# Three Strassen pieces instead of two in the first down product, nine low parts made by adding DMAs

## The chip, the cores and the metric

The kernel runs on one core of one Trainium2 chip. The metric is device time in microseconds (us) of one execution. Engine names are those of the profile: PE (matrix multiply), PEld (its weight load), DVE (vector), ACT (scalar), POOL (GpSimd), SP (the queue that issues most loads).

## The reference

One hybrid decoder layer for 256 tokens of width 1024 in float32: a SwiGLU feed-forward, a mixer (Mamba-2 and differential attention side by side), a second SwiGLU, each with RMSNorm before and after. What the change touches is the last product of the first feed-forward:

```python
D_MODEL, SEQ, D_FF = 1024, 256, 2816

def swiglu(x, w_gate, w_up, w_down):
    return (jax.nn.silu(x @ w_gate) * (x @ w_up)) @ w_down

h = h + 0.5 * rmsnorm(swiglu(rmsnorm(h, ffn1_pre_g[l]), ffn1_w_gate[l], ffn1_w_up[l], ffn1_w_down[l]),
                      ffn1_post_g[l])
```

So 256 x 2816 activations meet a 2816 x 1024 weight (the "down product"); the second feed-forward does the same with its own weights.

## The kernel before, in words

**Precision.** PE multiplies in a rounded float32 (`F32R`). Each weight and each activation is split into a high part (`hi`, the rounded value) and a low part (`lo`, the remainder), and each product is three: hi x hi, lo x hi, hi x lo. ACT makes `hi` by a cast, DVE makes `lo` by a subtraction (`whi`/`wlo` L250/L253 for ordinary pieces, `wqh`/`wql` L130/L135 for Strassen pieces).

**Weights.** They come in 1 MB pieces into three buffers called `raw` (SP issues the loads in order, L229); when the last reader of a buffer is done, the next piece is loaded. The split parts go into 4 KB buffers (`k4`, 29 of them). `take(ahead)` hands the split parts of the next unit to PE and first has the units ahead of it split: three pieces ahead, where a piece counts four and one Strassen product one, so twelve Strassen products ahead.

**The down product.** The 2816 rows are eleven pieces of 256 rows ("p"). An ordinary piece takes 24 matmuls of 128 x 512: two 128-row halves, two token blocks, two column halves, three terms. Two neighbouring pieces (512 rows) can be taken together as one "quad" (`q`) by Strassen's algorithm in Winograd's form: the 2 x 2 block product is made with seven products instead of eight, 42 matmuls instead of 48. For this a quad needs four sums of weight quarters (`wt`, L122, on DVE) and four sums of activations (`sums_of`, L607 to L610, made in the gate and up loop and split there). Three of the seven products (1, 2, 3) use a weight quarter as it is (`PLAIN`); four (5, 6, 7, 4) use a sum. `FIRST = (1, 2, 3, 5, 7, 6, 4)` is the order of the products of a quad, `LAST = (1, 6, 7, 2, 5, 3, 4)` that of the last one. The string `DOWN` says which pieces form quads: `"p q1 p p q2 p ppp"` in the first feed-forward (`f1`), `"q1 p q2 p q3 ppp"` in the second (`f2`). The last three pieces are held back (`TAIL = 3`): they are multiplied for token block 0 first, then for block 1, so that the norm of block 0 runs beside the matmuls of block 1.

**Order of the work.** PE follows the program in the stretches marked `own_order(PE)`, the tail of the down product among them; elsewhere a scheduler lays the instructions of each engine out when the program is built. On the chip each engine then follows its own list in order. After the last quad, `combine` (L654 to L657) adds the products: a copy of product 1 from its bank by ACT (`p1`, L657), then additions on DVE. `post_norm` scales the result (`og`, L541, with the gain row `pg`, loaded on POOL's queue at L554), POOL computes the reciprocal root (L447, L448), DVE updates `h` (L550), and PE transposes the new `h` for the next norm (`pu_mx`, L456).

Of the kernel before, what the change touches and what calls it, by code (L numbers as in the profile page):

```python
# [16 lines left out]
F32 = mybir.dt.float32  # L17
F32R = mybir.dt.float32r
AF = mybir.ActivationFunctionType
ALU = mybir.AluOpType  # L20
# [7 lines left out]
T = 256  # L28
# [16 lines left out]
QK_US = 2.4  # L45
GATE_US = 1.75
SSD_US = 1.55
DOWN = {"f1": "p q1 p p q2 p ppp", "f2": "q1 p q2 p q3 ppp"}
FIRST, LAST = (1, 2, 3, 5, 7, 6, 4), (1, 6, 7, 2, 5, 3, 4)
BREAK, STOP = object(), object()  # L50

# [2 lines left out]
def tile_hybrid_layer(ctx: ExitStack, tc: tile.TileContext, x, ffn1_pre_g, ffn1_w_gate, ffn1_w_up,  # L54
# [4 lines left out]
    nc = tc.nc  # L59
# [5 lines left out]
    def k4(shape, name, dt=F32):  # L65
        return sb.tile(shape, dt, tag="k4", name=name, bufs=K4_BUFS)
# [24 lines left out]
    last_lo = [None]  # L91

    class Quad:
# [3 lines left out]
        PLAIN = {1: 0, 2: 2, 3: 3}  # L97
        SUMS = {5: (1, 0), 6: (3, 5), 7: (3, 1), 4: (2, 6)}

        def __init__(self, i, products):  # L100
            self.i, self.sums, self.products = i, {}, products
            self.uses = [[p for p in products if p in (1, 5)], [p for p in products if p in (5, 7)],
                         [p for p in products if p in (2, 4)], [p for p in products if p in (3, 6, 7)]]

# [21 lines left out]
        def split(self, p):  # L126
            load_to(self.i + 2)
            hi = k4([P, 2, 512], f"wqh{self.i}{p}", F32R)
            src = self.quarter(self.PLAIN[p], p) if p in self.PLAIN else self.sum_of(p)
            nc.scalar.copy(hi, src)  # L130
            for later in self.products[self.products.index(p) + 1:][:1]:
                if later in self.SUMS:
                    self.sum_of(later)
            lo = k4([P, 2, 512], f"wql{self.i}{p}", F32R)
            last_lo[0] = nc.vector.tensor_sub(lo, src, hi.bitcast(F32)).ins  # L135
            self.give_back()
            return lambda kt: hi[:, kt, :], lambda kt: lo[:, kt, :]

# [2 lines left out]
    chunks, units = [], []  # L141
# [5 lines left out]
    def t_chunk(w, k0, c0):  # L147
        chunk(w[k0:k0 + D, c0:c0 + T].rearrange("(j p) c -> p j c", p=P), [P, KD, T])

    def s_chunk(w, k0, c0):  # L150
        chunk(w[k0:k0 + 512, c0:c0 + 512].rearrange("(j p) c -> p j c", p=P), [P, 4, 512])

    def n_chunk(w, k0):
        chunk(w[k0:k0 + 2 * P, :].rearrange("(j p) c -> p j c", p=P), [P, 2, D])

    def quad(w, k0, products):

        n = len(units)
        for k in (k0, k0 + 2 * P):
            n_chunk(w, k)  # L160
        del units[n:]
        q = Quad(len(chunks) - 2, products)
        units.extend((q, p) for p in products)


    down, QUADS = {}, {}
    for tag, plan in DOWN.items():
        QUADS[tag] = [int(c) for c in plan if c.isdigit()]
# [11 lines left out]
    def ffn_chunks(tag, wg, wu, wd):  # L180
        for w in (wg, wu):
            for k0 in (0, 512):
                s_chunk(w[0], k0, 0)
        for j in range(2, FF // T):
            t_chunk(wg[0], 0, j * T)
            t_chunk(wu[0], 0, j * T)
        for kind, j in down[tag]:
            if kind == "q":
                quad(wd[0], j * 2 * T, LAST if j == QUADS[tag][-1] else FIRST)
            else:  # L190
                n_chunk(wd[0], j * T)

    ffn_chunks("f1", ffn1_w_gate, ffn1_w_up, ffn1_w_down)
    for c in range(2):
        for k0 in (0, 512):
# [19 lines left out]
    for c in range(4):  # L215
        n_chunk(w_out[0], c * 2 * P)
    ffn_chunks("f2", ffn2_w_gate, ffn2_w_up, ffn2_w_down)

    raws, splits = [], []
    taken = [0]  # L220

    def load_to(n):
        while len(raws) < min(n, len(chunks)):
            i = len(raws)
            src, shape = chunks[i]
            r = sb.tile(shape, F32, tag="raw", name=f"raw{i}", bufs=RAW_BUFS)
            nj = shape[1] // 4 if i == 0 else shape[1] // 2 if i < 4 else shape[1]
            for j in range(0, shape[1], nj):
                nc.sync.dma_start(r[:, j:j + nj, :], src[:, j:j + nj, :])  # L229
            raws.append(r)  # L230
# [296 lines left out]
    def set_u(b, us):  # L527
        for q in range(2):
            split(*in_u(b)(q), us[q])
# [70 lines left out]
    def sums_of(g, even, odd):  # L600


        bs = (slice(0, P), slice(P, T))
        v = k4([P, 4, 2, P], f"sv{g}")
        hi, lo = ((k3 if g < 3 else k4)([P, 3, 2, P], f"s{n}{g}", F32R) for n in "hl")
        more = k2([P, 2, 2, P], f"s4{g}", F32R)
        nc.vector.tensor_tensor(v[:, 0], even[:, :, bs[1]], odd[:, :, bs[1]], ALU.add)  # L607
        nc.vector.tensor_sub(v[:, 2], even[:, :, bs[0]], even[:, :, bs[1]])
        nc.vector.tensor_sub(v[:, 1], v[:, 0], even[:, :, bs[0]])
        nc.vector.tensor_sub(v[:, 3], odd[:, :, bs[0]], v[:, 1])  # L610
        split(hi, lo, v[:, 0:3])
        split(more[:, 0], more[:, 1], v[:, 3])
        return ([hi[:, i] for i in range(3)] + [more[:, 0]], [lo[:, i] for i in range(3)] + [more[:, 1]])
# [724 lines left out]
    for c in range(4):  # L1338
# [3 lines left out]
        o = (c % 2) * 2  # L1342
# [134 lines left out]
```

## Time and profile before

| | |
|---|---|
| median of 3 runs | 738.33 us (738.31 to 738.46) |
| the profiled execution | 737.54 us, of which the span is 735.8 us |
| mean granted PE clock in it | 0.997 |
| busy: PE, DVE, ACT, POOL | 726.4, 591.9, 462.1, 38.6 us |
| first down product on PE | from 132.36 us |
| DMA: hardware queue q1, software queue q0 | 129.51 MB, 7.22 MB |

The span runs from the first to the last instruction. A matmul's listed duration includes its pipeline, so matmuls overlap: what a matmul costs is read from the distance of starts, or from the length of a stretch and the number of matmuls in it. `out<-in` names tiles with their numbers left out. "f1p" and "f2p" mark the banks of the two down products.

### The profile page before, as it was taken

The numbers are of one execution on the slowest core, as the hardware profiler recorded it, in microseconds if no ns is written. First come the engines' busy times: TensorE is split into PE (matmuls) and PEld (weight loads), VectorE is DVE, ScalarE is ACT, GpSimd is POOL, SyncE is SP. The second block draws the span as 40 slices with busy tenths as digits, with TensorE's granted clock in tenths as the row PEclk, the third lists the DMA queues.
The fourth block names the chain that finished last, engine by engine and source line by source line (L and its number), as shares of the span: only waits on it lengthen the run. The fifth ranks groups of instructions, "written<-read, shape, count | busy, mean of one in ns | idle before, by whom it ended". The sixth has DMA issues, their size and how long they took to land.

```text
span 735.8 us, 10869 instructions
## 1 busy us (share of the span) xinstructions
PE 726.4 (99%) x4211; PEld 628.1 (85%) x4211; DVE 591.9 (80%) x904; ACT 462.1 (63%) x777; POOL 38.6 (5%) x72
## 2 busy tenths in 40 slices
PE   8999999999999999999999999999999999999996
PEld 6888888888889999999888788888888888888874
DVE  7978768998677878787996998785784878779994
ACT  7657556665566565958975577782663657566562
POOL 2700000000300000000000000000010000000000
PEclk9999999999999999999999999999999999999998
DMA  8884674469353647567464664475470765664541
GB/s 299 229 261 150 218 229 171 155 216 348 118 172 117 201 143 226 192 188 226 146 219 154 202 222 138 152 238 191 127 241 34 229 199 153 222 217 143 188 168 57
DMA packets 94212, 137.96 MB, mean 187 GB/s; under 512 B 2684, under 2 KB 68304, under 8 KB 94160
## 3 DMA queue, kind: packets, MB, share of 16 engines
q1 hardware_dynamic: 91488, 129.51, 54.2%
q0 software_dynamic: 2368, 7.22, 3.1%
q8 instruction: 33, 0.54, 0.3%
q10 hardware_dynamic: 304, 0.53, 0.2%
q14 instruction: 19, 0.16, 0.1%
HBM read 136.17 MB, written 1.08 MB: 187 GB/s over the span
## 4 chain that ended last, share of the span: by engine, by line
PE 97%; DVE 2%; issue 1%; DMA 0%; ACT 0%; DVEq 0%
PE pup_f L316 9%; PE pg_f L316 9%; PE pgt L335 6%; PE pws L335 6%; PE acc_f1p L625 5%; PE acc_f2p L625 4%; PE pg_f L315 4%; PE pup_f L315 4%; PE pn_f L335 3%; PE pn_mx L335 3%; PE acc_mx L573 3%; PE pn_f L345 3%; PE pwd L335 3%; PE acc_f1p L573 3%; PE pz L302 2%; PE pxs L304 2%
## 5 line engine op out<-in xcount | busy, mean ns | idle before, releaser
L253 DVE TENSOR_TENSOR wlo<-raw,whi 128x1024 fp32r<-128x1024 f32 (+1 forms) x226 | 266.6, 1208 | 22.7 <-ACT whi L250 21.7
L250 ACT CAST whi<-raw 128x1024 fp32r<-128x1024 f32 (+1 forms) x225 | 226.2, 1044 | 18.1 <-DMA raw<-in_w_in_dram 3.8
L316 PE MATMUL pup_f<-u_f,whi 128*128 128x512 f32 x288 | 101.3, 396 | 0.0
L316 PE MATMUL pg_f<-u_f,whi 128*128 128x512 f32 x288 | 101.2, 396 | 0.0
L315 PE MATMUL pg_f<-u_f,wlo 128*128 128x256 f32 x252 | 70.6, 280 | 0.0
L315 PE MATMUL pup_f<-u_f,wlo 128*128 128x256 f32 x252 | 70.3, 279 | 0.0
L316 PEld LDWEIGHTS pup_f<-u_f,whi 128*128 128x128 f32 x288 | 52.8, 188 | 9.8
L316 PEld LDWEIGHTS pg_f<-u_f,whi 128*128 128x128 f32 x288 | 52.8, 188 | 9.6
L315 PEld LDWEIGHTS pg_f<-u_f,wlo 128*128 128x128 f32 x252 | 47.5, 188 | 1.7
L315 PEld LDWEIGHTS pup_f<-u_f,wlo 128*128 128x128 f32 x252 | 47.5, 189 | 1.6
L321 DVE TENSOR_TENSOR su_f<-pup_f,su_f 128x256 f32<-128x256 f32 x36 | 15.1, 420 | 26.0 <-ACT su_f L320 25.8
L130 ACT CAST wqh<-wt 128x1024 fp32r<-128x1024 f32 x20 | 21.0, 1052 | 23.2 <-DVE wt L122 23.2
L320 ACT COPY su_f<-pup_f 128x256 f32<-128x256 f32 x36 | 13.4, 373 | 35.1 <-PE pup_f L316 34.9
L335 PE MATMUL pgt<-whi,u_mx 128*128 128x512 f32 x128 | 33.1, 393 | 0.0
L301 PE MATMUL pxs<-u_mx,whi 128*128 128x256 f32 x128 | 31.7, 285 | 0.0
L302 PE MATMUL pz<-u_mx,whi 128*128 128x256 f32 x128 | 31.6, 284 | 0.0
L301 PE MATMUL pz<-u_mx,whi 128*128 128x256 f32 x128 | 31.6, 284 | 0.0
L302 PE MATMUL pxs<-u_mx,whi 128*128 128x256 f32 x128 | 31.4, 283 | 0.0
L335 PEld LDWEIGHTS pgt<-whi,u_mx 128*128 128x128 f32 x128 | 23.6, 188 | 5.4 <-issue 0.7
L1009 DVE SCALAR_TENSOR_TENSOR xs<-pxs,cols_b,xs 128x255 f32<-128x255 f32 (+2 forms) x48 | 21.9, 475 | 6.3 <-ACT xs L1006 5.9
L291 ACT CAST gh_f<-sg_f 128x512 fp32r<-128x512 f32 x18 | 11.2, 622 | 21.5 <-DVE sg_f L771 21.5
L302 PEld LDWEIGHTS pz<-u_mx,whi 128*128 128x128 f32 x128 | 24.5, 192 | 0.2 <-issue 0.2
(397 smaller groups left out, 1698.5 us busy)
## 6 DMA issues: line engine op xcount, KB each, us to landing
raw<-in_w_in_dram SPq DMA_DIRECT2D x40, 1024.0 KB, 5.4
raw<-in_ffn_w_down_dram SPq DMA_DIRECT2D x22, 1024.0 KB, 4.9
raw<-in_ffn_w_gate_dram SPq DMA_DIRECT2D x20, 1024.0 KB, 5.6
raw<-in_ffn_w_up_dram SPq DMA_DIRECT2D x20, 1024.0 KB, 5.4
raw<-in_ssd_w_branch_dram SPq DMA_DIRECT2D x8, 1024.0 KB, 5.3
acb<-acd POOLq DMA_DIRECT2D x8, 512.0 KB, 5.5
raw<-in_da_w_branch_dram SPq DMA_DIRECT2D x4, 1024.0 KB, 5.1
raw<-in_w_out_dram SPq DMA_DIRECT2D x4, 1024.0 KB, 5.0
```

The costliest lines, as they stand in the source:

```text
L130: nc.scalar.copy(hi, src)
L250: copy(hi[:, js, :], r[:, q * nj + j:q * nj + j + n, :])
L253: nc.vector.tensor_sub(lo[:, js, :], r[:, q * nj + j:q * nj + j + n, :], hi[:, js, :].bitcast(F32))
L301: nc.tensor.matmul(acc[m], wh(j)[:, cs], ah(k0 + j), start=first and j == ks[0], stop=False)
L302: nc.tensor.matmul(acc[m], wh(j)[:, cs], al(k0 + j), start=False, stop=False)
L315: nc.tensor.matmul(acc[:, :T], wl(j)[:, cs], ah(j), start=False, stop=False)
L316: nc.tensor.matmul(acc, wh(j)[:, cs], ahl(j), start=j == 0, stop=j == KD - 1)
L335: nc.tensor.matmul(acc, a(k0 + j), b(j), start=first and i == 0, stop=last and i == 11)
L345: nc.tensor.matmul(accs[b], x_(k0 + j), w_(j), start=first and j == 0 and w_ is wh and x_ is acts[b][0], stop=last and j == 3 and w_ is wl)
L573: nc.tensor.matmul(acc[b][q], x_[:, ts], w_(kt)[:, halves[q]], start=begin and i == 0 and kt == 0 and x_ is ah and w_ is wh, stop=i == n - ...
L625: nc.tensor.matmul(bank[p], x_, w_, start=p not in begun, stop=last and p in (1, 5, 6, 7))
L1009: nc.vector.scalar_tensor_tensor(dst[:, m, s:], acc[:, m, :T - s], cw(3 - s, c), dst[:, m, s:], ALU.mult, ALU.add)
```

## The change

`DOWN["f1"]` becomes the same plan as for `f2`: three quads instead of two, and the first quad at the start. So one more pair of ordinary pieces (48 matmuls) is taken as a quad (42), with its four weight sums and four activation sums, and the quads stand at other places.

For quads of `f1` the low part of the products 1, 2 and 3 is made in another way: ACT writes `-hi` into `lo` (one more activation of 128 x 1024 each), and a DMA on POOL's queue adds the weight quarter to it, read once more from DRAM (512 KB each, nine in all). The DVE subtraction of these nine is gone. The low parts of products 5, 6, 7 and 4 are still made by DVE, and the second feed-forward is not changed.

```diff
-DOWN = {"f1": "p q1 p p q2 p ppp", "f2": "q1 p q2 p q3 ppp"}
+DOWN = {"f1": "q1 p q2 p q3 ppp", "f2": "q1 p q2 p q3 ppp"}
+ADDING = ("f1",)
...
             lo = k4([P, 2, 512], f"wql{self.i}{p}", F32R)
-            last_lo[0] = nc.vector.tensor_sub(lo, src, hi.bitcast(F32)).ins
+            if self.adding and p in self.PLAIN:
+
+                nc.scalar.activation(lo, hi.bitcast(F32), AF.Copy, scale=-1.0)
+                j, o = divmod(self.PLAIN[p], 2)
+                nc.gpsimd.dma_start(lo, chunks[self.i + j][0][:, :, o * 512:(o + 1) * 512], accum_op=ALU.add)
+            else:
+                last_lo[0] = nc.vector.tensor_sub(lo, src, hi.bitcast(F32)).ins
             self.give_back()
...
-    def quad(w, k0, products):
+    def quad(w, k0, products, adding):
...
-                quad(wd[0], j * 2 * T, LAST if j == QUADS[tag][-1] else FIRST)
+                quad(wd[0], j * 2 * T, LAST if j == QUADS[tag][-1] else FIRST, tag in ADDING)
```

More of the change, by code (lines that the diff above doesn't have):

```diff
@@ L98, in tile_hybrid_layer, with __init__ @@
         SUMS = {5: (1, 0), 6: (3, 5), 7: (3, 1), 4: (2, 6)}
-        def __init__(self, i, products):
-            self.i, self.sums, self.products = i, {}, products
+        def __init__(self, i, products, adding):
+            self.i, self.sums, self.products, self.adding = i, {}, products, adding
             self.uses = [[p for p in products if p in (1, 5)], [p for p in products if p in (5, 7)],
@@ L161, in quad @@
         del units[n:]
-        q = Quad(len(chunks) - 2, products)
+        q = Quad(len(chunks) - 2, products, adding)
         units.extend((q, p) for p in products)
```

## The prediction

> **What bounds the kernel now.** I read the page first, then PE's waits, then PE stage by stage.
>
> ```profile
> PE 726.4 (99%) x4211; PEld 628.1 (85%) x4211; DVE 591.9 (80%) x904; ACT 462.1 (63%) x777; POOL 38.6 (5%) x72
> ...
> PE 97%; DVE 2%; issue 1%; DMA 0%; ACT 0%; DVEq 0%
> ```
>
> PE is busy for 99% of the span and holds 97% of the chain that ended last. PE's waits (us in total, times, longest):
>
> ```profile
> PE warm L411 <- POOL ident L397: 1.6, 1, 1.6
> PE pn_f L345 <- DVE raw_u L464: 0.3, 1, 0.3
> PE pn_f L345 <- DVE whi L250: 0.3, 1, 0.3
> PE pu_f L456 <- DMA h<-in_x_dram: 0.2, 1, 0.2
> ```
>
> These are all the waits it has, and none lies in a down product or a gate and up loop. So the weights are ready in time everywhere, a matmul less is worth its full pace, and any new wait of PE is a loss in full. Next, the windows of the first down product (second column the length, then PE, PEld, DVE, ACT, POOL busy, clock, DMA share, GB/s):
>
> ```profile
> 137.81:147.49 9.68, 9.68 (x43) 7.90 (x42) 9.19 (x9) 5.94 (x7) 0.00 (x0) 1.00 0.56 198
> 147.49:158.37 10.88, 10.88 (x49) 9.01 (x48) 9.60 (x9) 5.21 (x6) 0.00 (x0) 1.00 0.58 209
> ...
> 132.00:168.00 36.00, 36.00 (x159) 29.55 (x158) 33.08 (x33) 21.27 (x24) 0.53 (x1) 1.00 0.63 217
> 163.00:170.00 7.00, 7.00 (x32) 5.70 (x31) 7.00 (x8) 4.46 (x5) 0.53 (x1) 1.00 0.96 336
> ```
>
> The first row is a quad (42 matmuls), the second two ordinary pieces (48).
>
> **The matmuls.** A quad in place of two pieces: 10.88 - 9.68 = 1.20 us less on PE. That is all the change can give, since PE waits for nothing else that it could remove. It is 0.16% of the time, under the 0.2% (1.5 us) that a measurement of this kernel can tell from no change.
>
> **The engines beside PE.** Costs of one instruction:
>
> ```profile
> L250 ACT CAST whi<-raw 128x1024 fp32r<-128x1024 f32 x222 | 224.4, 1050 | 17.9 <-DMA raw<-in_w_in_dram 3.8 <-DMA raw<-in_ffn_w_down_dram 3.8 <-DMA raw<-in_ffn_w_up_dram 3.7
> L135 DVE TENSOR_TENSOR wql<-raw,wqh 128x1024 fp32r<-128x1024 f32 x15 | 18.2, 1219 | 3.6 <-ACT wqh L130 3.6
> ```
>
> DVE for the down weights: before 2 quads x 11 (4 sums, 7 lows) + 7 pieces x 2 = 36; after 3 x 8 + 5 x 2 = 34, two fewer, 2.4 us. ACT: before 2 x 7 + 7 x 2 = 28; after 3 x 10 + 5 x 2 = 40, twelve more, 12.6 us at 1.05 (the new copy is bounded by this cast of its shape). The stretch 132 to 168 leaves ACT 36 - 21.3 = 14.7 us idle, so ACT becomes nearly full but stays below PE. The third set of activation sums in the loop costs nothing: the second feed-forward's loop has the same three, and no row of PE's waits names it. If that cover failed it would cost at most its DVE time, some 3 us by my estimate.
>
> **What an adding DMA takes.** No run so far has one. The nearest rows (KB, us from issue to landing; the last two answers are the single transfers issued at 305.96 and 306.92):
>
> ```profile
> raw<-in_ffn_w_down_dram SPq DMA_DIRECT2D x22, 1024.0 KB, 4.9
> acb<-acd POOLq DMA_DIRECT2D x8, 512.0 KB, 5.5
> pg_mx<-in_mix_post_g_dram POOLq DMA_DIRECT2D x1, 512.0 KB, 3.7
> ```
> ```profile
> DMA to landing us min/median/max: 4.0/5.5/7.1
> ```
> ```profile
> 305.96 0.53 POOL L1071 DMA_DIRECT2D acb<-acd  x1 [16.16 <-PE pz L302]
> 306.92 0.53 POOL L1071 DMA_DIRECT2D acb<-acd  x1 [0.43 <-PE pz L302]
> ```
> ```profile
> DMA to landing us min/median/max: 4.0/4.0/4.0
> ```
> ```profile
> DMA to landing us min/median/max: 5.1/5.1/5.1
> ```
>
> A plain 512 KB on POOL's queue lands after 3.7 (quiet) to 7.1 (beside loads). An add also has to read what stands in the tile, so I take it as two passes. A second pass costs 4.9 - 3.7 = 1.2 us quiet; of the pair, the second landed at 312.0, the first at 310.0, so 2.0 us under load. Ends: 3.7 (adding costs nothing) and 7.1 + 2.0 = 9.1. Quiet two passes give 4.9, busy ones 4.0 + 2.0 = 6.0; I take 5.5, between them and the plain median. Below 3.7 nothing speaks for: it moves no less than the plain one.
>
> [...]
>
> **Third quad, product 3: a new chain.** In the order of instructions of the changed program, ACT's copy of product 1 out of its bank (`p1`, L657) stands ahead of the -hi copy for product 3 of the last quad, whose DMA waits for that copy. So this low part cannot be begun before PE has finished product 1 of the same quad. The second feed-forward has the same PE order (LAST: 1, 6, 7, 2, 5, 3, 4) and the same copy:
>
> ```profile
> 703.54 0.39 PE L625 MATMUL acc_f2p<-wql,gh_f 128*128 128x512 f32 x1
> ...
> 709.69 0.39 PE L625 MATMUL acc_f2p<-wql,s 128*128 128x512 f32 x1
> ```
> ```profile
> 703.97 0.59 ACT L657 COPY p_f<-acc_f2p 128x512 f32<-128x512 f32 x1 [0.38 <-PE acc_f2p L625]
> 704.45 1.05 ACT L130 CAST wqh<-raw 128x1024 fp32r<-128x1024 f32 x1
> ```
>
> Product 1 ends at 703.93, the copy starts at 703.97, the next ACT instruction (there the cast, here -hi) at 704.45 and ends at 705.5; the DMA is issued at about 705.6, and PE wants the low part at 709.69. That leaves 4.1 us. With 5.5 us PE waits 1.4 (ends 0 and 5.0). On POOL only the load of the gain row is queued behind it. It is read late in the tail and hidden: `pg` went out at 708.1 in the second feed-forward and was read at 718.5.
>
> ```profile
> L554 POOL DMA_DIRECT2D pg_f<-in_ffn_post_g_dram x2: 533/580/626, 163.0 to 708.1; - x2
> ```
> ```profile
> 718.53 0.69 DVE L541 TENSOR_TENSOR og_f<-p_f,pg_f 128x512 f32<-128x512 f32 x1
> ```
>
> **Second quad, products 1 to 3.** ACT starts them behind `gh_f` of the last loop step:
>
> ```profile
> 679.25 0.62 ACT L291 CAST gh_f<-sg_f 128x512 fp32r<-128x512 f32 x1 [2.98 <-DVE sg_f L771]
> 679.77 2.94 ACT L130 CAST wqh<-raw 128x1024 fp32r<-128x1024 f32 x3
> ```
> ```profile
> 690.48 0.39 PE L625 MATMUL acc_f2p<-wql,s 128*128 128x512 f32 x1
> ```
>
> DVE has three subtractions fewer ahead of this point, but it waits for casts that ACT now makes three copies later, so I leave the start where it is. Now six ACT instructions stand there at 0.98 us (2.94 / 3): the DMAs go out at about 681.7, 683.7 and 685.7. PE wants the third low part at 690.48, 4.8 us after. The three queue on one another: at two quiet passes of 1.2 us each, the last lands at 681.7 + 5.5 + 2 x 2.4 = 692.0, and PE waits 1.5 us. Ends: 0 (plain pace, 685.7 + 3.7 = 689.4) and 5.2 (two passes of 2.0 us each: 681.7 + 6.0 + 8.0 = 695.7). The first quad's adds have more room:
>
> ```profile
> 661.99 1.05 ACT L130 CAST wqh<-raw 128x1024 fp32r<-128x1024 f32 x1
> ```
> ```profile
> 675.36 0.39 PE L625 MATMUL acc_f2p<-wql,s 128*128 128x512 f32 x1
> ```
>
> The third cast starts at 661.99; with itself, three -hi copies and one `gh_f` (0.62) its DMA goes out by 666.8, 8.5 us before PE's use at 675.36: hidden up to that.
>
> **The tail.** DVE's order there changes: between the last addition of block 0 and the update of `h`, two `wlo` subtractions now stand where there was none.
>
> ```profile
> 181.99 0.68 DVE L785 TENSOR_TENSOR u_f<-acc_f1p,u_f 128x512 f32<-128x512 f32 x1
> 182.70 0.69 DVE L541 TENSOR_TENSOR og_f<-u_f,pg_f 128x512 f32<-128x512 f32 x1
> 184.60 1.41 DVE L550 SCALAR_TENSOR_TENSOR h<-og_f,rp_f,h 128x512 f32<-128x512 f32 x2 [1.21 <-POOL rp_f L448]
> ```
> ```profile
> 185.81 1.03 PE L456 MATMUL pu_mx<-ident,h 128*128 128x128 f32 x8
> ```
>
> Two at some 1.14 us (starts apart) are 2.3; the idle 1.2 before `h` hides half, and `h` is later by 1.1. Its second half is ready at 186.0 now and PE takes it up at about 186.3, so PE waits 0.8 us (ends 0 and 1.5, where a weight load is late too).
>
> **Sum.** -1.2 + 1.5 + 1.4 + 0.8 = +2.5 us. Against the profiled execution, 737.54, that is 740.0; the median lies 0.8 above it (738.33), so 740.8.
>
> **Rivals.**
> - *The adds land in time.* At 4.1 us or less neither place waits, and PE loses at most the 0.8 of the tail: 737.1 to 737.9, faster than before, by less than can be told. It is decided at product 3 of the last quad. For it: 3.7 for a quiet load and 4.0 for some beside others. Against it: the median of 5.5 and the second read. [...] 0.26.
> - *The DMA engines become the bound.* Each add at two busy passes; the share was 0.63 over the down product and 0.96 around 163 to 170, where the last adds meet the loads of the next pieces. Waits of 5.2 and 5.0, with 0.8 for the tail, give +9.8: up to 748. For it: the 0.96. Against it: over 132 to 168 a third of the engines' time is free. 0.17.
> - *It gives more than the matmuls*, by an easier tail: over 1.5 us less, 736.5. PE's waits leave no room for it. 0.04.
> - *The change does not do what it says*: the instruction lists show nine DMAs on POOL and the six matmuls gone, so I give it no chance of its own.
>
> **How the numbers follow.** The forecast's own case (adds of 4.3 to 6.5 us, waits at both places or at the last) has 0.53 and reaches from 738.3 to 743.5; its likeliest point is 740.8. A fifth of it lies under 739.8, within 0.2%. So same: 0.26 + 0.11 = 0.37; faster by over 0.2%: 0.04; slower: 0.42 + 0.17 = 0.59. The range for 8 in 10 takes in the rival below and half of the one above: 737.2 to 745.5.
>
> **What would show it.** In the profile after: waits of PE on a DMA into `wql` (`acc_f1p`, L625's successor), one at product 3 of the last quad with the DMA's issue right behind ACT's `p1` copy, and one in the second quad; an issue-to-landing time of the adding DMA over 4.1 us; DVE's `h` later against `u_f` in the tail, with PE waiting at `pu_mx`; a quad stretch of 9.7 us plus these waits. I am wrong if the adds land under 4 us, if the scheduler's lists leave `p1` free of that -hi copy, or if raw loads come late enough that ACT's casts and not the adds hold PE.

## The result, and the profile after

The changed kernel takes 746.16 us (median of 6 runs; the kernel before 738.24 in the same runs): a ratio of 1.0123, 95% interval 1.0098 to 1.0149. It is slower by 8 us where the forecast was 2.5 us (740.8, range to 745.5). The six runs went from 744.96 to 754.3 us; the longest had the lowest mean granted clock (0.988), the two shortest the highest (0.998). Its profiled execution took 746.76 us with a span of 745.1, 9.3 us more than the span of before. Lines of the changed program stand seven further down (L625 is L632 now).

The page of the kernel after (busy time, DMA queue of POOL, chain, issue to landing):

```profile
PE 728.6 (98%) x4205; PEld 628.3 (84%) x4205; DVE 592.8 (80%) x908; ACT 474.3 (64%) x791; POOL 50.7 (7%) x81
...
q0 software_dynamic: 4816, 11.94, 7.0%
...
PE 87%; issue 4%; DMA 3%; DVE 3%; POOL 1%; ACT 1%; SPq 0%; DVEq 0%; POOLq 0%; ACTq 0%
...
wql<-in_ffn_w_down_dram POOLq DMA_DIRECT2D x9, 512.0 KB, 7.6
```

The six matmuls are gone (4211 to 4205), yet PE is busy 2.2 us longer: some of its matmuls got slower (listed with 0.63 us instead of 0.39 between 157.17 and 159.73 us). The chain holds DMA now, and an adding DMA lands after a median of 7.6 us. PE's waits in the kernel after (us in total, times, longest):

```profile
PE acc_f1p L632 <- DMA wql<-in_ffn_w_down_dram: 6.5, 4, 1.8
PE warm L418 <- POOL ident L404: 1.6, 1, 1.6
PE pu_mx L463 <- DVE h L557: 0.8, 1, 0.8
```

Its timeline, the PE rows that waited:

```profile
149.45 0.50 PE L632 MATMUL acc_f1p<-wql,gh_f 128*128 128x512 f32 x1 [1.26 <-DMA wql<-in_ffn_w_down_dram]
...
152.80 0.50 PE L632 MATMUL acc_f1p<-wql,gh_f 128*128 128x512 f32 x1 [1.69 <-DMA wql<-in_ffn_w_down_dram]
...
156.23 0.50 PE L632 MATMUL acc_f1p<-wql,s 128*128 128x512 f32 x1 [1.78 <-DMA wql<-in_ffn_w_down_dram]
...
178.97 0.50 PE L632 MATMUL acc_f1p<-wql,s 128*128 128x512 f32 x1 [1.74 <-DMA wql<-in_ffn_w_down_dram]
...
194.59 1.32 PE L463 MATMUL pu_mx<-ident,h 128*128 128x128 f32 x8 [0.80 <-DVE h L557]
```

Three waits in the second quad (all three plain products), one at product 3 of the third, one in the tail: the places of the forecast, which had reckoned with one wait in the second quad. The second quad's three additions are issued 2.0 us apart and land after 8.2, 9.5 and 10.9 us:

```profile
141.24 1.19 POOL L140 DMA_DIRECT2D wql<-in_ffn_w_down_dram  x1 [13.77 <-ACT wql L138]
143.28 1.18 POOL L140 DMA_DIRECT2D wql<-in_ffn_w_down_dram  x1 [0.85 <-ACT wql L138]
145.30 1.19 POOL L140 DMA_DIRECT2D wql<-in_ffn_w_down_dram  x1 [0.84 <-ACT wql L138]
```

Between the first two, at 142.26 us, SP issues a plain load of 1 MB (`raw`), which lands after 8.6 us. What the forecast did not have is in the windows from the second of these waits on (length, PE, PEld, DVE, ACT, POOL busy, granted clock, DMA share, GB/s):

```profile
149.50:152.80 3.30, 1.61 (x7) 1.00 (x7) 3.28 (x3) 2.11 (x3) 0.00 (x0) 1.00 1.12 220
152.80:156.20 3.40, 1.65 (x6) 1.05 (x6) 2.46 (x3) 2.94 (x3) 0.00 (x0) 1.00 1.08 300
156.20:158.00 1.80, 1.77 (x5) 1.43 (x6) 0.59 (x1) 0.00 (x0) 1.18 (x1) 0.67 1.02 385
158.00:160.00 2.00, 2.00 (x6) 1.58 (x5) 1.86 (x2) 0.00 (x0) 0.00 (x0) 0.50 1.07 367
160.00:162.00 2.00, 2.00 (x9) 1.59 (x9) 1.60 (x2) 1.34 (x2) 0.00 (x0) 0.94 0.96 181
```

The DMA engines are full through the whole stretch, at only 220 GB/s in its first row (the loads alone moved 336 GB/s at a share of 0.96 before). And after the third wait PE's granted clock falls to 0.50. From 156.56 to 160.16 us PE starts 9 matmuls in 3.6 us instead of 2.0.

The loss up to the first matmul of the next projection (`pn_mx`, 190.82 us before, 199.89 after, so +9.1) adds up from the distances of starts: -1.2 matmuls, +5.5 second quad, +1.5 lower clock, +2.0 third quad, +1.1 tail, together 8.9. The second quad's 5.5 is more than its three waits (4.7 us), since a wait is counted from the listed end of the matmul before it (0.39 us, where starts are 0.23 apart) and PE starts slowly behind each (the next start comes 0.33 to 0.34 us later, not 0.23); the tail's 1.1 is its wait of 0.80 and a slow restart of 0.3 (the eight `pu_mx` take 1.32 us, 1.03 before).

### The profile page after: what moved, and what is told of

It is laid out like the page before. It is cut to its first block, busy times and chain, and to the rows that moved or that the text cites. A ratio compares the mean times of both kernels' runs of the same rounds, so it can differ in the third digit from the quotient of the medians.

```text
span 745.1 us, 10902 instructions
## 1 busy us (share of the span) xinstructions
PE 728.6 (98%) x4205; PEld 628.3 (84%) x4205; DVE 592.8 (80%) x908; ACT 474.3 (64%) x791; POOL 50.7 (7%) x81
## 4 chain that ended last, share of the span: by engine, by line
PE 87%; issue 4%; DMA 3%; DVE 3%; POOL 1%; ACT 1%; SPq 0%; DVEq 0%; POOLq 0%; ACTq 0%
PE pup_f L323 8%; PE pg_f L323 8%; PE pws L342 6%; PE pgt L342 6%; PE pg_f L322 4%; PE pup_f L322 4%; PE acc_f2p L632 3%; PE pn_f L342 3%; PE acc_mx L580 3%; PE pn_mx L342 3%; PE pn_f L352 3%; PE pwd L342 3%; DMA wql<-in_ffn_w_down_dram 2%; PE pz L309 2%; PE pxs L311 2%
## 5 line engine op out<-in xcount | busy, mean ns | idle before, releaser
L260 DVE TENSOR_TENSOR wlo<-raw,whi 128x1024 fp32r<-128x1024 f32 (+1 forms) x222 | 262.2, 1209 | 20.2 <-ACT whi L257 19.0
L257 ACT CAST whi<-raw 128x1024 fp32r<-128x1024 f32 (+1 forms) x221 | 222.4, 1044 | 16.0 <-DMA raw<-in_w_in_dram 4.7
L142 DVE TENSOR_TENSOR wql<-wt,wqh 128x1024 fp32r<-128x1024 f32 x24 | 29.3, 1222 | 11.5 <-ACT wqh L131 11.3
L131 ACT CAST wqh<-wt 128x1024 fp32r<-128x1024 f32 x24 | 25.1, 1051 | 19.3 <-DVE wt L123 16.8
```

Of the source, the lines that this page charges most:

```text
L257: copy(hi[:, js, :], r[:, q * nj + j:q * nj + j + n, :])
L260: nc.vector.tensor_sub(lo[:, js, :], r[:, q * nj + j:q * nj + j + n, :], hi[:, js, :].bitcast(F32))
```

## The experiments

Theory: the additions land late, the waits pull the clock down, and the tail adds one us. Rivals: the third quad itself costs it; or it is the traffic, and the adding is not to blame.

| | what | median | ratio to before, 95% |
|---|---|---|---|
| E1 | three quads, no adding | 739.86 | 1.0028 (1.0016 to 1.0040) |
| E2 | nine DMAs copy instead of add | 743.71 | 1.0075 (1.0061 to 1.0089) |
| E3 | second quad without adding | 744.33 | 1.0080 (1.0065 to 1.0096) |
| E4 | as E3, and product 3 of the third | 739.85 | 1.0026 (1.0017 to 1.0035) |
| E5 | E1, tail put in the old order | 739.82 | 1.0021 (1.0013 to 1.0030) |
| E6 | E5, first quad adding | 739.48 | 1.0018 (1.0004 to 1.0033) |
| E7 | two quads, old plan, adding | 740.68 | 1.0035 (1.0024 to 1.0047) |
| E8 | all nine adding, spread | 743.85 | 1.0071 (1.0056 to 1.0087) |
| E9 | E5, both blocks' tail | 739.09 | 1.0011 (1.0002 to 1.0020) |
| E10 | E9, first quad adding | 738.76 | 1.0008 (0.9999 to 1.0018) |

**E1, three quads without adding.**

```diff
-ADDING = ("f1",)
+ADDING = ()
```

> Three quads, all lo parts made by VectorE's subtractions, no adding DMA. Theory (late additions, the clock drop that follows them, and a small tail): nothing waits for an addition, the granted clock stays at 1.00 near 156 to 160 us; 746.8 less 5.5 (second quad), 1.5 (clock) and 2.0 (third quad) is 737.8 with the tail of 1.1 kept, plus whatever VectorE's nine more subtractions of about 1.1 us each delay; 737.5 to 740. Rival one (the third quad itself, its copies or the tail, costs it): 743 or more. Rival two (the traffic on the queues, not the adding): as the first, 737.5 to 740, since the traffic goes too.

739.86 us: 6.3 of the 8 us go with the adding, and the first rival is out. The theory and the second rival have the same band here, and it holds 739.86; E2 has to part them. But the third quad does not give its 1.2 us either; the kernel is 1.7 us slower than the kernel before. PE's longest new wait in the profile of E1, and the POOL rows ahead of it:

```profile
183.11 2.12 POOL L454 TENSOR_SCALAR rp_f<-sp_f 128x1 f32<-128x1 f32 x1 [14.21 <-ACT jp_f L449]
185.31 0.57 POOL L455 TENSOR_TENSOR rp_f<-rp_f,nhalf 128x1 f32<-128x1 f32 x1
```
```profile
186.72 1.32 PE L463 MATMUL pu_mx<-ident,h 128*128 128x128 f32 x8 [1.67 <-DVE h L557]
```

The same POOL step in the kernel before, on as many elements:

```profile
183.60 0.31 POOL L447 TENSOR_SCALAR rp_f<-sp_f 128x1 f32<-128x1 f32 x1 [20.07 <-ACT jp_f L442]
183.99 0.57 POOL L448 TENSOR_TENSOR rp_f<-rp_f,nhalf 128x1 f32<-128x1 f32 x1
```

POOL worked on one column for 2.12 us instead of 0.31. DVE worked without a pause from 182.10 to 185.04 (`wlo`, `og`, `wlo`), and POOL's step ended at 185.23; in the kernel before DVE was idle at that point. `h` then waited another 0.87 us for POOL. So the two `wlo` that stand in the tail now may cost it twice: on DVE, and through POOL. In the kernel after, POOL's two steps took 0.90 and 1.39 us, and there too `h` waited for POOL last:

```profile
193.79 1.42 DVE L557 SCALAR_TENSOR_TENSOR h<-og_f,rp_f,h 128x512 f32<-128x512 f32 x2 [0.47 <-POOL rp_f L455]
```

This became a question of its own (E5). E1 also waits in the second feed-forward, whose plan is not changed:

```profile
PE acc_f2p L580 <- DVE wlo L260: 0.7, 2, 0.5
```

E1 is 1.2 us behind the kernel before at the first matmul of the projection (192.04 against 190.82) and 2.0 us at the end of the span; these two waits are most of the difference. Why DVE is late there too was not traced.

**E2, copying instead of adding.** The nine DMAs stay where they are, with their waits and sizes, but the low part is then the weight itself: `-hi` is overwritten and nothing is added. POOL's time to issue one changes with it (0.71 us instead of 1.19).

```diff
-                nc.gpsimd.dma_start(lo, ..., accum_op=ALU.add)
+                nc.gpsimd.dma_start(lo, ...)
```

> The nine DMAs stay where they are, with their waits, sizes and issues, but copy instead of adding, so the addition of the negated hi part is left out. Theory: a plain 512 KB transfer takes about 1.7 us of all 16 engines where an adding one takes 3.3, so the DMA share between 149 and 163 us falls under 1 and landings fall from 5.7 to 10.9 us to about 4 to 6.5; the second quad's waits fall from 5.5 us to under 2, the clock does not drop, 738.5 to 741.5. Rival two (the issue and the chain copy, addition, subtraction cost it, not the adding): 744.5 to 747.

743.71 us, between the bands of theory and rival. Queue q0 of the page before, then of the page of E2, with its issue to landing:

```profile
q0 software_dynamic: 2368, 7.22, 3.1%
```
```profile
q0 software_dynamic: 4816, 11.94, 5.2%
...
wql<-in_ffn_w_down_dram POOLq DMA_DIRECT2D x9, 512.0 KB, 4.9
```

Same packets, same bytes as after, and less engine time. Over what q0 took before (3.1% of 735.8 = 22.8 us of all 16 engines), nine copies take 38.6 - 22.8 = 15.8 us, 1.76 each; nine additions took 7.0% of 745.1 = 52.2, less 22.8 = 29.4, 3.26 each: 1.86 times as much. The forecast had reckoned an addition as two passes of a copy: that was the author's estimate, and the engine time comes near it (1.86); what the addition reads and writes is not shown. The second quad's waits are gone (under 2 us was expected), but the total misses the theory's band: at product 3 of the third quad a copy issued at 166.73 us landed after 8.3, beside loads (windows of E2, then PE's row):

```profile
171.00:175.10 4.10, 0.00 (x0) 0.00 (x0) 2.45 (x3) 1.53 (x3) 0.00 (x0) 0.93 1.06 384
175.10:178.00 2.90, 2.89 (x7) 2.31 (x8) 2.87 (x4) 0.63 (x1) 0.00 (x0) 0.51 1.03 358
```
```profile
175.11 0.79 PE L632 MATMUL acc_f1p<-wql,s 128*128 128x512 f32 x1 [4.34 <-DMA wql<-in_ffn_w_down_dram]
```

So there are two causes. Back to back, it is the adding that makes the DMAs late (second quad, where the copies landed after 3.8, 5.8 and 5.4 us and the additions after 8.2, 9.5 and 10.9); where plain loads fill the engines (share 1.06 at 384 GB/s), a copy comes late as well (8.3). The clock falls here too, to 0.51, after a single gap of 4.34 us.

**E3 and E4, fewer additions.** E3 makes the second quad's low parts by DVE (pieces 25 and 26), E4 also product 3 of the third quad (28):

```diff
-            if self.adding and p in self.PLAIN:
+            if self.adding and p in self.PLAIN and self.i != 25:                              # E3
+            if self.adding and p in self.PLAIN and self.i != 25 and (self.i, p) != (28, 3):   # E4
```

> The second quad's three lo parts are made by VectorE again; first and third quad keep their six adding DMAs. Theory: the second quad's 5.5 us of waits and the 1.5 us of lower clock go, 746.8 - 7.0 = 739.8, 738.8 to 741. Rival one (the third quad itself): 744 or more. Rival two (adding anywhere costs it): the first quad's and the third quad's shares stay, 742 to 744.

> As the one before, and product 3 of the third quad has its lo part by VectorE too; five adding DMAs are left, those that nothing waited for. Theory: also the 2.0 us wait before the third quad's last product goes, 737.8, 737 to 739, by which it would be within 0.2% of the kernel before, with the tail of 1.1 us left against the 1.2 us of matmuls saved. Rival one: 744 or more. Rival two: 741 to 743.

PE's waits for additions in the profile of E3, the window behind them, and the wait in E4:

```profile
169.10 0.50 PE L632 MATMUL acc_f1p<-wql,gh_f 128*128 128x512 f32 x1 [1.22 <-DMA wql<-in_ffn_w_down_dram]
174.72 0.50 PE L632 MATMUL acc_f1p<-wql,s 128*128 128x512 f32 x1 [2.58 <-DMA wql<-in_ffn_w_down_dram]
```
```profile
174.70:178.00 3.30, 3.28 (x14) 2.72 (x15) 3.07 (x5) 0.00 (x0) 0.00 (x0) 1.00 1.04 401
```
```profile
170.13 0.50 PE L632 MATMUL acc_f1p<-wql,gh_f 128*128 128x512 f32 x1 [1.57 <-DMA wql<-in_ffn_w_down_dram]
```

Both expectations were too low; E3's median even lies in the band of the rival that blames the third quad itself (744 or more). E4 speaks against that rival: it keeps the third quad and is at 739.85. Without the second quad's waits PE arrives earlier at the third, and there an addition that had been in time is late (product 2, landing after 7.0 us in E3 and 7.3 in E4, 5.7 in the kernel after), and that of product 3 takes 8.1 us in E3 (5.7 in the kernel after): the wait moves to what comes next. E3's profiled execution took 742.42 us; in its other runs (743.0 to 745.4) the mean clock was lower, 0.993 to 0.995 against 0.998, so the profile explains its median only in part. E4 keeps one late addition (1.57), a wait of 0.8 at the start of the kernel and the tail's 0.8.

**E5, the tail in the old order.** E1, and the two `wlo` are put behind `h` of block 0 by an order among DVE's instructions:

```diff
-                nc.vector.tensor_sub(lo[:, js, :], ...)
+                m = nc.vector.tensor_sub(lo[:, js, :], ...)
+                if behind_h[0] is not None and len(splits) > behind_h[1]:
+                    tc.add_manual_dep(m.ins, behind_h[0], order, reason="behind h")
...
+        if tag == "f1" and b == 0:
+            behind_h[:] = [m.ins.name, len(splits) + 1]
...
```

> Three quads, all lo parts by VectorE, no adding DMA, and the two wlo that VectorE worked between its last addition of block 0 and h are put behind h, as they stood in the kernel before. Theory (those two subtractions cost the tail twice: 1.2 us of VectorE ahead of the addition, and GpSimd's small steps of rp_f, which took 2.12 and 0.57 us beside them instead of 0.31 and 0.57): rp_f's first step is back near 0.3 us, TensorE's wait of 1.67 us for h and its 0.3 us of slow restart go, the span falls by 1.5 to 2.0 us, 737.9 to 738.4. Rival (the tail is late because the third quad leaves VectorE behind, wherever the two stand): the wait stays over 1 us or returns before the projection's first product, 739.3 to 740.

POOL in the profile of E5, and PE's new wait:

```profile
183.39 0.31 POOL L456 TENSOR_SCALAR rp_f<-sp_f 128x1 f32<-128x1 f32 x1 [14.34 <-ACT jp_f L451]
183.78 0.57 POOL L457 TENSOR_TENSOR rp_f<-rp_f,nhalf 128x1 f32<-128x1 f32 x1
```
```profile
200.38 1.09 PE L465 MATMUL pu_mx<-ident,un_mx 128*128 128x128 f32 x8 [1.43 <-DVE un_mx L510]
```

The mechanism held: POOL's step is back at 0.31 us, no wait for `h` is left, and the projection starts at 190.5 us, 0.3 before the kernel before. The gain did not: the subtractions moved stand ahead of block 1's `h` now, and PE waits 1.43 us for `un_mx`, which is made from it; the 0.7 us in the second feed-forward are there as in E1. The median stays (739.82). DVE is simply behind, and pushing its work back moves the wait (E9 goes on from here).

That it is behind shows in the windows of 168 to 178 us, before and then E1:

```profile
168.00:178.00 10.00, 10.00 (x46) 8.27 (x45) 8.09 (x9) 6.16 (x7) 0.00 (x0) 1.00 0.96 336
```
```profile
168.00:178.00 10.00, 9.93 (x44) 7.85 (x43) 10.00 (x11) 6.36 (x7) 0.53 (x1) 1.00 0.94 346
```

DVE is full (10.00 of 10.00, before 8.09); and the loads of the next weights, issued from 165.59 us on before, are issued from 171.20 on in E1.

**E6, adding in the first quad only**, on top of E5 (`... and self.i == 22`).

> As the one before, and the first quad's three lo parts by adding DMAs, which nothing waited for in any run so far. Theory: three subtractions less on VectorE and no wait on an addition: 737 to 738.4, at or just under the kernel before. Rival (adding costs wherever it stands): 740 or more.

739.48 us. No addition is waited for. DVE has three subtractions less, but still PE waits 0.41 us for `h` and 1.29 for `un_mx`: neither expectation is met, and it differs from E5 by 0.3 us only, with intervals that overlap.

**E7, adding without the third quad.** The old plan `"p q1 p p q2 p ppp"` with `ADDING = ("f1",)`.

> The old plan of two quads and its order, with their six lo parts by adding DMAs: the adding without the third quad. Theory (what costs is the adding DMA's landing beside other traffic): TensorE waits for additions again, above all in the last quad, where plain loads fill the DMA engines from 162 us on; 2 to 5 us of waits, 740 to 744. Rival (the third quad costs it): 737.5 to 738.7.

PE's waits in the profile of E7:

```profile
PE acc_f1p L632 <- DMA wql<-in_ffn_w_down_dram: 0.5, 1, 0.5
PE pu_mx L463 <- DVE h L557: 0.4, 1, 0.4
```

740.68 us, inside the theory's band, but with 0.5 us of waits for additions instead of 2 to 5. At the projection's first product E7 is 1.7 us behind the kernel before (192.5 against 190.8), at the end of the span 2.8. Its last store is issued 1.75 us later than before (734.20 against 732.45) and takes 2.1 us to land in both, so the last us of the difference stands behind the last store, and what it is stays open. What is shown is that adding gains nothing on the old plan either.

**E8, the additions spread.** All nine, but every quad of the first down product takes its products in the order `LAST`.

```diff
-                quad(wd[0], j * 2 * T, LAST if j == QUADS[tag][-1] else FIRST, tag in ADDING)
+                quad(wd[0], j * 2 * T, LAST if tag in ADDING or j == QUADS[tag][-1] else FIRST, tag in ADDING)
...
-            for p in LAST if last else FIRST:
+            for p in LAST if last or tag in ADDING else FIRST:
```

> All nine additions, but all three quads of the first down product take their products in the last quad's order, so that the three plain products, and their additions, stand some 4 to 8 us apart instead of 2. Theory (three additions of 3.3 us of all DMA engines each, issued 2 us apart, queue behind one another): the second quad's landings fall from 8.2 to 10.9 us to 5.5 to 8, its waits from 5.5 us to under 2.5, no lower clock there; the third quad's 2 to 4 us and the tail stay; 740 to 743.5. Rival (additions are late whatever their distance): 745 to 748.

PE's waits in the profile of E8 on the first, second and third quad's product 3, and in the tail:

```profile
141.69 0.50 PE L632 MATMUL acc_f1p<-wql,s 128*128 128x512 f32 x1 [1.59 <-DMA wql<-in_ffn_w_down_dram]
158.19 0.50 PE L632 MATMUL acc_f1p<-wql,s 128*128 128x512 f32 x1 [1.10 <-DMA wql<-in_ffn_w_down_dram]
174.46 0.50 PE L632 MATMUL acc_f1p<-wql,s 128*128 128x512 f32 x1 [0.97 <-DMA wql<-in_ffn_w_down_dram]
191.84 1.32 PE L463 MATMUL pu_mx<-ident,h 128*128 128x128 f32 x8 [2.55 <-DVE h L557]
```

The second quad's waits fall to 1.10 us, its landings to 7.4, 5.6 and 8.7 us, and the clock stays at 1.00 in all three quads. The first quad waits now (1.59), and the tail for 2.55 us: 743.85, a little over the band. The spacing of the additions matters; it does not save the change.

**E9 and E10, the next two `wlo` behind block 1's `h` too**, without additions (E9) and with the first quad's (E10), on top of E5:

```diff
-        if tag == "f1" and b == 0:
-            behind_h[:] = [m.ins.name, len(splits) + 1]
+        if tag == "f1":
+            behind_h[:] = [m.ins.name, len(splits) + (b == 0)]
...
+        ready(1)
         split_to(ahead_of(taken[0], AHEAD))
-        ready(1)
+        behind_h[0] = None
```

> Three quads, all lo parts by VectorE, and now also the next two wlo are put behind the second block's h, since with only the first pair moved TensorE waited 1.43 us at the second pu_mx for un_mx. Theory (VectorE is simply behind at the end of the third quad, and each block's h has to be put ahead of weights that are wanted later): that wait falls under 0.5 us, the span falls by about 1.3 us, 738.2 to 738.8, within 0.2% of the kernel before. Rival (the two subtractions are needed where they stood): another wait of 1 us or more in the projection, 739.3 to 740.

> As the one before, with the first quad's three lo parts by adding DMAs. Theory: three subtractions less ahead of the same place, 0.4 us of wait for h left and the 1.29 us for un_mx gone: 737.6 to 738.4, no slower than the kernel before and perhaps 0.1% faster. Rival: adding DMAs give VectorE back time that it cannot use here, 738.6 to 739.6.

PE's waits that are left beyond the kernel's start, in E10:

```profile
PE pu_mx L465 <- DVE h L559: 0.4, 1, 0.4
...
PE pn_mx L344 <- DVE wlo L260: 0.2, 1, 0.2
```

738.76 us, 0.08% over the kernel before with an interval that holds no change; E9 lies at 0.11% (739.09, between its two bands); E10 lies in its rival's band. The wait for `un_mx` is gone in both. E10 is the best version found, and none beats the kernel before: its 1.2 us of matmuls are just paid for.

## Why the prediction was wrong in size

- *Matmuls, -1.2.* Right in kind: 4205 for 4211. In E1 the stretch from the start of `pup_f` at 104.4 us to the last start of block 0's product is 80.24 us with a stall of some 0.3 in it; before it is 81.19.
- *First quad hidden.* Right: no wait in the kernel after, and none in E6.
- *Third quad, product 3, +1.4.* Right in the chain: the addition was issued at 173.19 us behind ACT's `p1` copy (171.34) and the -hi copy (171.83), landed after 5.7 us (5.5 taken), and cost 2.0. That the landing fits is in part luck: the loads of the next weights went out only from 177.38 us, after the second quad had held PE up. In E3, where it does not, they go out from 170.77, the same addition takes 8.1 us, and PE waits 2.58.
- *Tail, +0.8.* The place and the size are right, 0.80 of wait and a slow restart of 0.3; the mechanism is right by half. `h` starts 4.04 us after the start of block 0's last addition (189.75), 2.61 before: 1.4 later, where 1.1 was reckoned from DVE alone. The last 0.47 us of it DVE waits for POOL, whose steps took 0.90 and 1.39 us instead of 0.31 and 0.57. The working lacked that DVE held POOL up there, so the exact 0.80 is luck.
- *Second quad, +1.5: the step that failed.* The first of three additions was to land 5.5 us after its issue, the other two 2.4 us apart behind it, at two quiet passes of 1.2 us each. The first took 8.2 us, and they landed at 149.4, 152.8 and 156.2 us, 3.4 apart, about the 3.26 us of all 16 engines that one addition takes by the shares. So the last landed 15.0 us after the first issue where 10.3 were reckoned: 2.7 us more for the first landing, 2.0 for the distances. The DMA engines were full by then (share 1.12), with the additions and with the plain load issued at 142.26. The busy pass (2.0 us) stood in the same paragraph as the upper end, 5.2 us, and 5.5 came. I took the quiet row for a place where the additions themselves make the traffic.
- *The clock: missing.* The sum put it at nothing. No row of before showed a granted clock under 1.00 in a product, and PE never waited there. It cost 1.5 us more in the profiled run; the other runs have no trace of it.
- Rival "DMA engines become the bound" (0.17) is what happened in the second quad and, in this kernel, not in the third. The rival "adds land in time" needed 4.1 us; the least in the kernel after was 5.7.

With 5.5 and 1.5 in place of 1.5 and 0 the sum gives 746.3 for the median, against 746.16. So close a fit is luck: the third quad and the tail took 0.9 us more than their terms, and the terms were read in the profiled run (746.76), not in the median one.

## What to carry to other kernels

An adding DMA took 1.86 times the engine time of a copy here: cost several of them, issued close together, by the engines' own pace (3.26 us of all 16 for one), with the loads that run beside them, and not by a quiet landing. Where PE is at 99%, three subtractions taken off DVE gave 0.3 us at most (E6 against E5, E10 against E9, neither clear of noise), while every late operand cost its wait and in two profiles the clock as well (0.50 in the kernel after, 0.51 in E2). On a critical chain, look for subtractions on DVE beside small POOL steps (0.31 us became 2.12 in E1 and was 0.31 again in E5).

## What the runs showed that I had not expected

- **The clock fell after several short waits.** In E2 one gap of 4.34 us was followed by 2.9 us at 0.51. In E3 two, of 1.22 and 2.58 and ending at 169.1 and 174.7, left it at 1.00. In the kernel after no wait was over 1.8 us, but three, of 1.26, 1.69 and 1.78 within 8 us, PE being busy for 1.61 of 3.30 and 1.65 of 3.40 us between them, brought it to 0.50. In E8 three of 1.59, 1.10 and 0.97, some 16 us apart, left it at 1.00. So one gap of 2.58 us with another ahead of it did not lower the clock and one of 4.34 did; in the kernel after the clock fell without a single gap of that length. That the half-idle stretch did it is read from this one profile and not tested by itself.
- **DVE held POOL up.** A step of 0.31 us took 2.12 beside `wlo` subtractions and 0.31 again with them moved (E1, E5). In E1 POOL's step ended 0.2 us after a row of DVE instructions (`wlo`, `og`, `wlo`, 182.10 to 185.04 us), not after the first of them. By what means they hold it up is not shown.
- **Issuing an addition takes POOL 1.19 us**, a copy of the same tile 0.71 (medians in the kernel after and in E2).
